# Layer 0's first norm: root on ScalarE, norm weights through TensorE, loads in another order

## The chip, the core and the metric

The kernel runs on one core of one Trainium2 chip. The metric is device time in microseconds (us) of one execution, given as the median of several runs. TensorE (PE, its weight loads PEld) multiplies matrices, VectorE (DVE) and ScalarE (ACT) do elementwise work, GpSimd (POOL) does some more of it, SyncE (SP) issues most DMAs. Every engine takes its instructions strictly in the order of the program and waits on semaphores for the others.

## The reference, cut to what matters

Two layers over 1024 tokens of width 1024: layer 0 mixes by neighbourhood attention, layer 1 by grouped-query attention. Each starts with an RMS norm and a projection. The change touches only the first norm and what surrounds it:

```
def rms_norm(x, g):
    y = x * lax.rsqrt(mean(x * x, axis=-1, keepdims=True) + NORM_EPS)
    return y * g

for i in range(DEPTH):
    h = rms_norm(x, norm_g[i])          # i == 0: the norm of this case
    y = mixer_a(h, ...)                 # layer 0: q, k, v, gate = split(h @ w_in, 4)
    ...
```

## The kernel before

All matrix products are done in three parts: every f32 operand is split into a high part (`wh`, `HTh`) and the rest (`wl`, `HTl`), and `split3` multiplies high by high, high by low and low by high. `mixer_a` begins with a prologue that this case is about. The 1024 tokens are eight tiles `X[t]` of 128 tokens by 1024 columns. For each tile:

- `square` (L720, ACT) makes the sum of squares of each token in a column of `stat`; an ACTIVATE and a short read of the accumulator.
- `newton` (L723) and `rsqrt_ops` (L308) make the reciprocal root on DVE: a shift and a subtraction on the bits for a first guess, then three Newton steps, 10 or 13 instructions of one to four columns each. They run for tile 0, tile 1, tiles 2 and 3, and tiles 4 to 7 as groups; `weave` lays them between other work.
- `scale` (L734) multiplies the tile by root and norm weight. Tiles 0, 1, 2, 4 and 6 do it in one DVE instruction against `gt`, the norm weights copied to all 128 partitions by a DMA of 512 KB (L745). Tiles 3, 5 and 7 do it in two: ACT by the root (L738), POOL by the weights (L739).
- `to_ht` (L422) transposes the tile in two halves of four PE transposes (L427) into a PSUM tile `t`, copies it to `HTh` (L428, ACT) and the rest to `HTl` (L429, DVE).
- `v_items` (L582) projects it to v for the first four heads: two halves of four column blocks, 12 matmuls each (L302), first against weight unit `("av", 0, 0)`, then `("av", 0, 1)`. The evacuation of the PSUM tile `d` takes ACT (L587) and DVE (L588).

The class `Weights` (`WQ`) brings weights in: `stage` issues the DMA of a unit of 512 KB into one of two staging tiles (L202, SP), `pump` copies it to `wh` on ACT (L217) and leaves the subtraction for `wl` (L218, DVE) to `settle`. The order of all of it is the order in which this code is written (the schedule is manual): each call appends to its engine's queue. The SP queue holds tile 0, the 512 KB of norm weights, tile 1, two weight units, tiles 2 to 7. After the eight tiles come `qk_items(0)` (512-column matmuls) and the attention loop, whose scores take the PSUM pool `psS`.

Of the kernel before, what the change touches and what calls it, by code (L numbers as in the profile page):

```python
# [11 lines left out]
F32 = mybir.dt.float32  # L12
# [24 lines left out]
DT = (5, 2)  # L37
FIN = (4, 4)
HOLD = 2
DP = 1  # L40
KD, KS = 3, 4
QD = (2, 5, 8)
# [42 lines left out]
def lay_out(inp):  # L85
    g = {k: np.asarray(v) for k, v in inp.items()}
    W = np.empty((len(UNIT), 128, 1024), np.float32)

    def put(keys, cols, per):
        blk = cols.reshape(cols.shape[0] // 128, 128, -1).transpose(1, 0, 2)  # L90
        for u, key in enumerate(keys):
            W[UNIT[key]] = blk[:, u * per:(u + 1) * per].reshape(128, -1)

    aq, ak, av, ag = np.split(g["a_w_in"][0], 4, axis=1)
    for h in range(16):
        s = slice(h * HD, (h + 1) * HD)
        put([("aqk", h)], np.concatenate([aq[:, s], ak[:, s]], axis=1), 8)
    for q in range(4):
        put([("av", q, 0), ("av", q, 1)], av[:, q * 256:(q + 1) * 256], 4)
    bw = g["b_w_in"][0]  # L100
    bq, bk, bv, bg = bw[:, :1024], bw[:, 1024:1280], bw[:, 1280:1536], bw[:, 1536:]
    for p in range(8):
        s = slice(p * 128, (p + 1) * 128)
        put([("ag", p)], ag[:, s], 8)
        put([("bg", p)], bg[:, s], 8)
    for i in range(4):
        put([("bq", i, 0), ("bq", i, 1)], bq[:, i * 256:(i + 1) * 256], 4)
    for i in range(2):
# [12 lines left out]
    rpb = np.zeros((16, 31, 32), np.float32)  # L121
    rpb[:, 8:23, :31] = g["a_rpb"][0]

    gains = np.stack([g["norm_g"][0], g["ple_norm_g"][0], g["norm_g"][1], g["ple_norm_g"][1], g["final_norm_g"]])

    r = np.arange(128) // 8
    c = np.arange(128) % 8
    rs = np.clip(r - 4, 0, 8)
    rowok = (r[None, :] >= rs[:, None]) & (r[None, :] < rs[:, None] + 8)
    left = rowok & (c[None, :] >= c[:, None])  # L130
    right = rowok & (c[None, :] < c[:, None])
    ok = np.stack([rowok, left, rowok, right, rowok], axis=1)
    mask = np.where(ok, 0.0, BIG).astype(np.float32)

    inv = np.power(np.float32(10000.0), -np.arange(16, dtype=np.float32) * np.float32(2.0) / np.float32(32.0)).astype(np.float32)
    row = r.astype(np.float32)[:, None, None] + np.zeros((1, 8, 1), np.float32)
    col = (8 * np.arange(8)[None, :] + c[:, None]).astype(np.float32)[:, :, None]
    ar = (row * inv).astype(np.float32)
    ac = (col * inv).astype(np.float32)
    cosT = np.concatenate([np.cos(ar), np.cos(ar), np.cos(ac), np.cos(ac)], axis=2).astype(np.float32)  # L140
    sinT = np.concatenate([-np.sin(ar), np.sin(ar), -np.sin(ac), np.sin(ac)], axis=2).astype(np.float32)

    def swap(v):
        return v.reshape(2, 2, 16)[:, ::-1].reshape(64)

    bqn, bkn = g["b_q_norm"][0], g["b_k_norm"][0]
    hg = np.stack([bqn, swap(bqn), bkn, swap(bkn)])
    return {
        "x": tokens(g["x"][0]), "wts": W, "rpb": rpb, "gains": gains, "hgains": hg,
        "mask": mask, "rope": np.stack([cosT, sinT], axis=1),  # L150
    }


@with_exitstack
def trunk(ctx, tc, x, wts, rpb, gains, hgains, mask, rope, out):
    nc = tc.nc
    sync, act, dve, pool, pe = nc.sync, nc.scalar, nc.vector, nc.gpsimd, nc.tensor

# [218 lines left out]
            items.append((f, 650.0 * (k1 - k0)))  # L377
        return items

    def proj_N(keys, t, ncol, alloc, evac, release=(), kstep=None):  # L380
        kstep = kstep or KN
        st = {}
        items = []
        per = 1024 // ncol
        nk = per * len(keys)
        for k0, k1 in chunks(nk, kstep):
            def f(k0=k0, k1=k1):
                if k0 == 0:
                    st["ps"] = alloc()
                for k in range(k0, k1):  # L390
                    wh, wl = WQ.get(keys[k // per])
                    c = slice((k % per) * ncol, (k % per + 1) * ncol)
                    split3(st["ps"], HTh[:, t, k, :], HTl[:, t, k, :], wh[:, c], wl[:, c], k == 0, k == nk - 1)
                if k1 == nk:
                    if release:
                        WQ.done(*release)
                    evac(st["ps"])
            items.append((f, 3 * (ncol / 2.4 + 3) * (k1 - k0)))
        return items
# [160 lines left out]
    def mixer_a():  # L560
        with ExitStack() as es:
# [17 lines left out]
            QS, KA, KB, TB, RS, SP, OP, UT = {}, {}, {}, {}, {}, {}, {}, {}  # L579
            later = Later()  # L580

            def v_items(qd, t):  # L582
                keys = [("av", qd, 0), ("av", qd, 1)]

                def evac(ps):
                    v = ps.rearrange("p (h d) -> p h d", h=4)
                    act.activation(V[:, t, :, 0:64], v, AF.Copy)  # L587
                    dve.tensor_tensor(V[:, t, :, 64:128], v, V[:, t, :, 0:64], ALU.subtract)  # L588
                return [d[0] for d in proj_N(keys, t, 256, valloc, evac, release=keys if t == NT - 1 else ())]

            def qk_evac(h, hf):
                def evac(ps):
# [115 lines left out]
            e2 = es.enter_context(ExitStack())  # L708
            ini = e2.enter_context(tc.tile_pool(name="ini", bufs=1))
            X = [ini.tile([128, D], F32, name=f"X{t}") for t in range(NT)]  # L710
            gt = ini.tile([128, D], F32, name="gain")
            junk = ini.tile([128, D], BF16, name="junk")
            stat = one.tile([128, 3, 8], F32, name="stat")
            wk = one.tile([128, 24], F32, name="wki")
# [1 line left out]
            def load(t):  # L716
                sync.dma_start(X[t], x[t])
# [1 line left out]
            def square(t):  # L719
                act.activation(junk, X[t], AF.Square, accum_out=stat[:, 0, t:t + 1])  # L720

            def newton(a, b):
                ms = stat[:, 1, a:b]  # L723
                return [lambda: dve.tensor_scalar(ms, stat[:, 0, a:b], 1.0 / D, EPS, op0=ALU.mult, op1=ALU.add)] \
                    + rsqrt_ops(stat[:, 2, a:b], ms, wk)

            def weave(ops, fs):
                per = -(-len(ops) // len(fs))
                for i, f in enumerate(fs):
                    for o in ops[i * per:(i + 1) * per]:  # L730
                        o()
                    f()

            def scale(t):  # L734
                if t % 2 == 0 or t == 1:
                    dve.scalar_tensor_tensor(X[t], X[t], stat[:, 2, t:t + 1], gt, op0=ALU.mult, op1=ALU.mult)
                else:
                    act.activation(X[t], X[t], AF.Copy, scale=stat[:, 2, t:t + 1])  # L738
                    pool.tensor_tensor(X[t], X[t], gt, ALU.mult)  # L739

            def ht(t):
                return [lambda c=c: to_ht(psT, t, X[t], (c,)) for c in range(2)]

            load(0)
            sync.dma_start(gt, bcast(gains, 0, D))  # L745
            load(1)
            WQ.stage(True)
            for t in range(2, NT):
                load(t)
            U = dram.tile([16, 8, 31, 24], F32, name="U")  # L750
            square(0)
            square(1)
            weave(newton(0, 1), [lambda: scale(0)])
            WQ.pump(True)
            WQ.pump(True)
            vs = [v_items(0, t) for t in range(NT)]
            weave(newton(1, 2), ht(0))
            scale(1)
            square(2)
            square(3)  # L760
            vs[0][0]()
            weave(newton(2, 4), ht(1))
            scale(2)
            scale(3)
            square(4)
            square(5)
            square(6)
            vs[0][1]()
            sync.dma_start(MK, mask)
            for c in range(8):  # L770
                sync.dma_start(U[:, c], rpb[:, :, 7 - c:31 - c])
            for t in range(1, NT):
                vs[t][0]()
                if t + 1 < NT:
                    weave(newton(4, 8) if t == 2 else [], ht(t + 1))
                if t == 1:
                    square(7)
                if t in (2, 3):
                    scale(2 * t)
                    scale(2 * t + 1)  # L780
                vs[t][1]()
                if t == 6:
                    load_u(0)
# [526 lines left out]
    dense_phase(1)  # L1310


NAMES = ["x", "wts", "rpb", "gains", "hgains", "mask", "rope"]


# [13 lines left out]
```

## Time and profile before

| | us |
|---|---|
| median of 3 runs (1569.87 to 1572.43) | 1572.35 |
| the profiled execution | 1569.38 |
| its span, first to last instruction | 1567.6 |
| PE busy in the span | 1522.6 |
| ACT busy in the span | 871.6 |

The span is read as follows: each row of the timeline gives a start and a duration from the span's start, the engine, the line, what is written from what, and in brackets how long the engine sat idle before and what ended that. Windows give the busy time of each engine in a stretch.

### The profile page before, as it was taken

How to read it: one execution, taken by the hardware profiler on the slowest of the kernel's cores; microseconds unless marked ns; L12 is line 12 of the kernel's file. 1: busy time of each engine (PE TensorE's matmuls, PEld its weight loads, DVE VectorE, ACT ScalarE, POOL GpSimd, SP SyncE). 2: the span in 40 equal slices, each digit the busy share in tenths (PEclk: the TensorE clock that was granted, in tenths of full speed). 3: DMA queues.
4: the chain of work that ended last, by engine and by line, in shares of the span. 5: the costliest groups of instructions: out<-in, count | busy, mean ns of one | idle time of the engine just before them, and what ended most of it. 6: DMA issues, size and time to landing. Idle time of an engine off the chain costs nothing.

```text
span 1567.6 us, 24292 instructions
## 1 busy us (share of the span) xinstructions
PE 1522.6 (97%) x9048; PEld 1328.5 (85%) x9048; DVE 1025.5 (65%) x2062; ACT 871.6 (56%) x1744; POOL 277.3 (18%) x372
## 2 busy tenths in 40 slices
PE   6999999999999999999999999999999999999997
PEld 5888988988988788888988889989899888788886
DVE  6576576477477436547877776777777877625636
ACT  6465465466366522433566776666667767622422
POOL 2111121122112010000312132443132200000023
PEclk9999999999999999999999999999999999999999
DMA  8212122132123972132210111102111213651213
GB/s 273 78 41 74 49 84 78 34 98 78 35 85 95 340 241 67 62 139 90 74 48 21 38 51 41 58 25 68 37 33 42 75 42 112 225 202 54 74 55 128
DMA packets 89861, 138.84 MB, mean 89 GB/s; under 512 B 16912, under 2 KB 55952, under 8 KB 89744
## 3 DMA queue, kind: packets, MB, share of 16 engines
q1 hardware_dynamic: 85136, 122.62, 24.1%
q10 hardware_dynamic: 4608, 14.68, 2.6%
q8 instruction: 71, 1.16, 0.3%
q14 instruction: 46, 0.38, 0.1%
HBM read 104.65 MB, written 36.15 MB: 90 GB/s over the span
## 4 chain that ended last, share of the span: by engine, by line
PE 40%; DVE 7%; ACT 3%; issue 2%; DMA 0%; ACTq 0%; SPq 0%; POOL 0%; DVEq 0%; POOLq 0%
PE d L302 21%; PE o L302 7%; PE t L1084 5%; PE s L302 5%; DVE PTl L1087 2%; DVE mn L1068 1%; ACT PTh L1086 1%; DVE wl L218 1%; PE t L427 1%; ACT wh L217 1%; PE t L1038 0%; ACT P L1074 0%; DVE QS L1048 0%; DVE ss L915 0%; DVE KB L979 0%
## 5 line engine op out<-in xcount | busy, mean ns | idle before, releaser
L302 PE MATMUL d<-wh,HTh 128*128 128x256 f32 (+1 forms) x1096 | 372.5, 340 | 4.6 <-ACT HTh L428 2.1
L302 PE MATMUL d<-wh,HTl 128*128 128x256 f32 (+1 forms) x1096 | 365.8, 334 | 1.6 <-DVE HTl L429 1.5
L302 PE MATMUL d<-wl,HTh 128*128 128x256 f32 (+1 forms) x1096 | 365.3, 333 | 0.0
L1087 DVE TENSOR_TENSOR PTl<-t,PTh 128x512 fp32r<-128x512 f32 x256 | 164.5, 684 | 115.4 <-ACT PTh L1086 114.9
L302 PEld LDWEIGHTS d<-wh,HTh 128*128 128x128 f32 x1096 | 207.9, 190 | 28.0 <-ACT HTh L428 2.7
L302 PEld LDWEIGHTS d<-wh,HTl 128*128 128x128 f32 x1096 | 207.8, 190 | 24.0 <-DVE HTl L429 2.3
L302 PEld LDWEIGHTS d<-wl,HTh 128*128 128x128 f32 x1096 | 208.1, 190 | 21.4
L302 PE MATMUL d<-HTh,wh 128*128 128x512 f32 x504 | 205.9, 409 | 0.0
L302 PE MATMUL d<-HTh,wl 128*128 128x512 f32 x504 | 197.7, 392 | 0.0
L302 PE MATMUL d<-HTl,wh 128*128 128x512 f32 x504 | 197.7, 392 | 0.0
L1074 ACT ACTIVATE P<-s,mn 128x1024 f32<-128x1024 f32 x128 | 142.8, 1115 | 66.2 <-DVE mn L1068 65.1
L302 PE MATMUL o<-PTl,V 128*128 128x256 f32 (+2 forms) x672 | 174.2, 290 | 3.2 <-DVE PTl L1087 2.0
L302 PE MATMUL o<-PTh,V 128*128 128x256 f32 (+2 forms) x672 | 173.0, 288 | 2.3 <-ACT P L1074 1.1
L1086 ACT ACTIVATE PTh<-t 128x512 fp32r<-128x512 f32 x256 | 139.9, 593 | 45.9 <-PE t L1084 45.0
L1068 DVE TENSOR_REDUCE mn<-s 128x1 f32<-128x1024 f32 x128 | 154.8, 1209 | 10.8 <-PE s L302 10.7
L1084 PE MATMUL t<-ident,P 128*128 128x128 f32 x1024 | 137.2, 275 | 8.0 <-DVE PTl L1087 6.6
L218 DVE TENSOR_TENSOR wl<-wstage,wh 128x1024 fp32r<-128x1024 f32 x89 | 115.0, 1298 | 40.9 <-ACT wh L217 40.4
L302 PEld LDWEIGHTS o<-PTl,V 128*128 128x128 f32 x672 | 127.9, 190 | 10.6 <-DVE PTl L1087 6.4
L302 PEld LDWEIGHTS o<-PTh,V 128*128 128x128 f32 x672 | 127.7, 190 | 8.1 <-issue 1.5
L1084 PEld LDWEIGHTS t<-ident,P 128*128 128x128 f32 x1024 | 114.9, 140 | 23.1 <-DVE PTl L1087 16.2
L302 PE MATMUL s<-KA,QS 128*128 128x512 f32 (+2 forms) x384 | 133.6, 402 | 0.0
L302 PE MATMUL s<-KB,QS 128*128 128x512 f32 (+2 forms) x384 | 121.8, 371 | 0.0
(179 smaller groups left out, 2446.8 us busy)
## 6 DMA issues: line engine op xcount, KB each, us to landing
wstage<-in_wts SPq DMA_DIRECT2D x92, 512.0 KB
X<-in_x SPq DMA_DIRECT2D x16, 512.0 KB
pp<-ppD SPq DMA_DIRECT2D x32, 256.0 KB
rb<-rD SPq DMA_DIRECT2D x56, 128.0 KB
ppD<-th SPq DMA_DIRECT2D x20, 256.0 KB
xD<-X SPq DMA_DIRECT2D x8, 512.0 KB
X<-xD SPq DMA_DIRECT2D x8, 512.0 KB
yD0h<-rb SPq DMA_DIRECT2D x14, 256.0 KB
```

The costliest lines, as they stand in the source:

```text
L217: act.activation(hi, s, AF.Copy)
L218: self.rest = lambda: dve.tensor_tensor(lo, s, hi, ALU.subtract)
L302: pe.matmul(ps, a, b, start=first, stop=last, skip_group_check=True)
L427: pe.transpose(ps[:, k], xn[:, (4 * c + k) * 128:(4 * c + k + 1) * 128], ident)
L1068: dve.tensor_reduce(mn, ps, axis=AX.X, op=ALU.min)
L1074: act.activation(p, ps, AF.Exp, bias=mn, scale=-1.0, accum_out=RS[h, hf][:, t:t + 1])
L1084: pe.transpose(ps[:, i], p[:, k * 128:(k + 1) * 128], ident)
L1086: act.activation(PTh[:, ks, c], ps, AF.Copy)
L1087: dve.tensor_tensor(PTl[:, ks, c], ps, PTh[:, ks, c], ALU.subtract)
```

## The change

The first norm takes another way to the root. `chain(a, b)` replaces `newton` and `weave`: ACT computes Ln(sum / 1024 + eps) and Exp of -0.5 times that, DVE adds one Newton step (three or four instructions). It runs once for each of tiles 0 to 3 and once for tiles 4 and 5 and for tiles 6 and 7. `scale` is two DVE instructions of 512 columns for every tile, and reads the norm weights from two PSUM tiles that PE fills: a DMA of 128 x 8 values (`gT`, on ACT's queue), spread over the partitions by eight transposes. `warm` adds eight transposes of the identity before these and eight behind. SP loads tile 0, weight unit 0, tile 1, weight unit 1, tiles 2 to 7. For tiles 0 and 1 the 12 matmuls of a half are ordered by part (`thirds`). Layers, loops and DMAs behind the eight tiles stay in their order on every engine.

```diff
+        "gain0": gains[0].reshape(8, 128).T,
...
-    def proj_N(keys, t, ncol, alloc, evac, release=(), kstep=None):
+    def proj_N(keys, t, ncol, alloc, evac, release=(), kstep=None, thirds=False):
...
+                for i in range(3 if thirds else 0):
+                    for k in range(k0, k1):
...
+                        a, b = ((HTh, wh), (HTh, wl), (HTl, wh))[i]
+                        mm(st["ps"], a[:, t, k, :], b[:, c], i == 0 and k == 0, i == 2 and k == nk - 1)
...
+            def chain(a, b):
+                n = b - a
+                ss, y, r = stat[:, 0, a:b], stat[:, 1, a:b], stat[:, 2, a:b]
+                h, w = wk[:, a:b], wk[:, 8 + a:8 + b]
+                act.activation(w, ss, AF.Ln, scale=1.0 / D, bias=eps)
+                act.activation(y, w, AF.Exp, scale=-0.5)
+                dve.tensor_scalar(h, ss, -0.5 / D, -0.5 * EPS, op0=ALU.mult, op1=ALU.add)
...
+                dve.scalar_tensor_tensor(r, w, 1.5, y, op0=ALU.add, op1=ALU.mult)
+
+            def scale(t, cs=(0, 1)):
+                for c in cs:
+                    w = slice(512 * c, 512 * c + 512)
+                    dve.scalar_tensor_tensor(X[t][:, w], X[t][:, w], stat[:, 2, t:t + 1], gain[c], op0=ALU.mult, op1=ALU.mult)
...
+            def warm(ps, n):
+                for k in range(n):
+                    pe.transpose(ps[:, k % 4 * 128:k % 4 * 128 + 128], ident, ident)
...
+            act.dma_start(gT, gain0)
+            hold = WQ.hold
+            WQ.hold = ("av", 0, 1)
             load(0)
-            sync.dma_start(gt, bcast(gains, 0, D))
+            WQ.stage(True)
             load(1)
+            WQ.hold = hold
             WQ.stage(True)
             for t in range(2, NT):
                 load(t)
...
+            dve.memset(eps, EPS)
+            act.activation(junk[:, :1], eps, AF.Ln)
+            gain = [psS.tile([128, 512], F32, name="s") for c in range(2)]
+            warm(gain[0], WARM[0])
+            for k in range(KC):
+                pe.transpose(gain[k // 4][:, k % 4 * 128:k % 4 * 128 + 128], gT[:, k:k + 1].to_broadcast([128, 128]), ident)
+            warm(pd.tile([128, 512], F32, name="d"), WARM[1])
...
             square(0)
+            chain(0, 1)
+            scale(0)
+            split()
+            ht(0, (0,))
             square(1)
+            chain(1, 2)
+            ht(0, (1,))
             scale(1)
+            vs[0][0]()
+            split()
             square(2)
+            chain(2, 3)
+            ht(1)
+            scale(2)
             square(3)
+            chain(3, 4)
+            vs[0][1]()
+            vs[1][0]()
+            ht(2, (0,))
+            vs[1][1]()
+            ht(2, (1,))
             scale(3)
...
-            for t in range(1, NT):
+            for t in range(2, NT):
                 vs[t][0]()
                 if t + 1 < NT:
-                    weave(newton(4, 8) if t == 2 else [], ht(t + 1))
+                    ht(t + 1)
...
                 if t in (2, 3):
-                    scale(2 * t)
-                    scale(2 * t + 1)
+                    square(2 * t)
+                    square(2 * t + 1)
+                    chain(2 * t, 2 * t + 2)
+                if t + 2 < NT:
+                    scale(t + 2)
                 vs[t][1]()
```

ACT's queue at tiles 0 and 1. `X_107` and `X_108` are the tiles 0 and 1, `X_109` is tile 2; `junk,stat` is the square, `wki<-stat,eps` the logarithm, `stat<-wki` the exponential, ACT_TABLE_LOAD an instruction that the build puts in for the function that follows. Before:

```order
L720 ACTIVATE junk,stat<-X_107 128x1024
L720 ACTIVATE junk,stat<-X_108 128x1024
L217 ACTIVATE wh_146<-wstage 128x1024
L217 ACTIVATE wh_152<-wstage 128x1024
L428 ACTIVATE HTh<-t 128x512 x2
L720 ACTIVATE junk,stat<-X_109 128x1024
```

And of the change:

```order
L729 ACTIVATE junk,stat<-X_107 128x1024
L735 ACTIVATE wki<-stat,eps 128x1
L736 ACT_TABLE_LOAD
L736 ACTIVATE stat<-wki 128x1
L219 ACTIVATE wh_171<-wstage 128x1024
L436 ACTIVATE HTh<-t 128x512
L729 ACTIVATE junk,stat<-X_108 128x1024
L735 ACT_TABLE_LOAD
L735 ACTIVATE wki<-stat,eps 128x1
L736 ACT_TABLE_LOAD
L736 ACTIVATE stat<-wki 128x1
L436 ACTIVATE HTh<-t 128x512
```

Tile 0's second half (the last row) now stands behind tile 1's square, two table loads, the logarithm and the exponential.

ACT's queue at tiles 4 to 7 (`X_111` to `X_114`), from the square of tile 4. Before, the squares of tiles 4 to 6 follow each other, and one root serves all four:

```order
L720 ACTIVATE junk,stat<-X_111 128x1024
L720 ACTIVATE junk,stat<-X_112 128x1024
L720 ACTIVATE junk,stat<-X_113 128x1024
L587 ACTIVATE V<-d 128x4x64
L428 ACTIVATE HTh<-t 128x512 x2
L720 ACTIVATE junk,stat<-X_114 128x1024
```

And of the change:

```order
L729 ACTIVATE junk,stat<-X_111 128x1024
L729 ACTIVATE junk,stat<-X_112 128x1024
L735 ACT_TABLE_LOAD
L735 ACTIVATE wki<-stat,eps 128x2
L736 ACT_TABLE_LOAD
L736 ACTIVATE stat<-wki 128x2
L595 ACTIVATE V<-d 128x4x64
L436 ACTIVATE HTh<-t 128x512 x2
L729 ACTIVATE junk,stat<-X_113 128x1024
```

The same group of two squares, two loads, logarithm and exponential follows once more for tiles 6 and 7. In all ACT has one ACT_TABLE_LOAD before and twelve now, the first of them in front of the logarithm of `eps` at the start; none stands behind the eight tiles.

DVE's queue of the change at the root of tiles 6 and 7, up to the scaling of tile 5 (`X_112`):

```order
L596 TENSOR_TENSOR V<-d,V 128x4x64
L437 TENSOR_TENSOR HTl<-t,HTh 128x512 x2
L737 TENSOR_SCALAR wki<-stat 128x2
L742 TENSOR_TENSOR wki<-stat 128x2
L743 TENSOR_TENSOR wki<-wki 128x2
L744 SCALAR_TENSOR_TENSOR stat<-wki,stat 128x2
L749 SCALAR_TENSOR_TENSOR X_112<-X_112,stat,s 128x512 x2
```

Tile 5 is scaled behind the Newton step of tiles 6 and 7, which reads their exponential.

More of the change, by code (lines that the diff above doesn't have):

```diff
@@ L39 @@
 HOLD = 2
+WARM = (8, 8)
 DP = 1
@@ L150, in lay_out, with trunk @@
         "mask": mask, "rope": np.stack([cosT, sinT], axis=1),
+        "gain0": gains[0].reshape(8, 128).T,
     }
 @with_exitstack
-def trunk(ctx, tc, x, wts, rpb, gains, hgains, mask, rope, out):
+def trunk(ctx, tc, x, wts, rpb, gains, hgains, mask, rope, gain0, out):
     nc = tc.nc
@@ L389, in f @@
                     st["ps"] = alloc()
-                for k in range(k0, k1):
+                for i in range(3 if thirds else 0):
+                    for k in range(k0, k1):
+                        wh, wl = WQ.get(keys[k // per])
+                        c = slice((k % per) * ncol, (k % per + 1) * ncol)
+                        a, b = ((HTh, wh), (HTh, wl), (HTl, wh))[i]
+                        mm(st["ps"], a[:, t, k, :], b[:, c], i == 0 and k == 0, i == 2 and k == nk - 1)
+                for k in range(k0, k1) if not thirds else ():
                     wh, wl = WQ.get(keys[k // per])
@@ L580, in mixer_a, with v_items @@
             later = Later()
-            def v_items(qd, t):
+            def v_items(qd, t, thirds=False):
                 keys = [("av", qd, 0), ("av", qd, 1)]
@@ L588, in evac @@
                     dve.tensor_tensor(V[:, t, :, 64:128], v, V[:, t, :, 0:64], ALU.subtract)
-                return [d[0] for d in proj_N(keys, t, 256, valloc, evac, release=keys if t == NT - 1 else ())]
+                return [d[0] for d in proj_N(keys, t, 256, valloc, evac, release=keys if t == NT - 1 else (), thirds=thirds)]
             def qk_evac(h, hf):
@@ L710, in mixer_a @@
             X = [ini.tile([128, D], F32, name=f"X{t}") for t in range(NT)]
-            gt = ini.tile([128, D], F32, name="gain")
+            gT = ini.tile([128, 8], F32, name="gT")
+            eps = ini.tile([128, 1], F32, name="eps")
             junk = ini.tile([128, D], BF16, name="junk")
@@ L720, in square @@
                 act.activation(junk, X[t], AF.Square, accum_out=stat[:, 0, t:t + 1])
[L722 to L732, printed above, removed]
@@ L734, in scale @@
-            def scale(t):
-                if t % 2 == 0 or t == 1:
-                    dve.scalar_tensor_tensor(X[t], X[t], stat[:, 2, t:t + 1], gt, op0=ALU.mult, op1=ALU.mult)
-                else:
[L738 to L742, printed above, removed]
+            def chain(a, b):
[5 more added lines that the diff above has]
+                dve.tensor_scalar(h, ss, -0.5 / D, -0.5 * EPS, op0=ALU.mult, op1=ALU.add)
+                w = wk[:, 16 + a:16 + b]
+                if n == 1:
+                    dve.scalar_tensor_tensor(w, y, h, y, op0=ALU.mult, op1=ALU.mult)
+                else:
+                    dve.tensor_tensor(w, y, y, ALU.mult)
+                    dve.tensor_tensor(w, w, h, ALU.mult)
+                dve.scalar_tensor_tensor(r, w, 1.5, y, op0=ALU.add, op1=ALU.mult)
@@ new lines, in scale, with ht, split @@
+            def scale(t, cs=(0, 1)):
+                for c in cs:
+                    w = slice(512 * c, 512 * c + 512)
+                    dve.scalar_tensor_tensor(X[t][:, w], X[t][:, w], stat[:, 2, t:t + 1], gain[c], op0=ALU.mult, op1=ALU.mult)
+            def ht(t, cs=(0, 1)):
+                to_ht(psT, t, X[t], cs)
+            def warm(ps, n):
+                for k in range(n):
+                    pe.transpose(ps[:, k % 4 * 128:k % 4 * 128 + 128], ident, ident)
+            def split():
+                WQ.pump(True)
+                WQ.settle()
@@ L744, in mixer_a @@
+            U = dram.tile([16, 8, 31, 24], F32, name="U")
+            act.dma_start(gT, gain0)
+            hold = WQ.hold
+            WQ.hold = ("av", 0, 1)
             load(0)
-            sync.dma_start(gt, bcast(gains, 0, D))
+            WQ.stage(True)
             load(1)
+            WQ.hold = hold
             WQ.stage(True)
@@ L749, in mixer_a @@
                 load(t)
-            U = dram.tile([16, 8, 31, 24], F32, name="U")
+            dve.memset(eps, EPS)
[5 more added lines that the diff above has]
+            warm(pd.tile([128, 512], F32, name="d"), WARM[1])
+            vs = [v_items(0, t, t < 2) for t in range(NT)]
             square(0)
+            chain(0, 1)
+            scale(0)
+            split()
+            ht(0, (0,))
             square(1)
[L753 to L757, printed above, removed]
+            chain(1, 2)
+            ht(0, (1,))
             scale(1)
+            vs[0][0]()
+            split()
             square(2)
+            chain(2, 3)
+            ht(1)
+            scale(2)
             square(3)
-            vs[0][0]()
-            weave(newton(2, 4), ht(1))
-            scale(2)
+            chain(3, 4)
[4 more added lines that the diff above has]
+            ht(2, (1,))
             scale(3)
[L765 to L768, printed above, removed]
             sync.dma_start(MK, mask)
@@ L771, in mixer_a @@
                 sync.dma_start(U[:, c], rpb[:, :, 7 - c:31 - c])
-            for t in range(1, NT):
+            for t in range(2, NT):
                 vs[t][0]()
                 if t + 1 < NT:
-                    weave(newton(4, 8) if t == 2 else [], ht(t + 1))
-                if t == 1:
-                    square(7)
+                    ht(t + 1)
                 if t in (2, 3):
-                    scale(2 * t)
-                    scale(2 * t + 1)
+                    square(2 * t)
[3 more added lines that the diff above has]
+                    scale(t + 2)
                 vs[t][1]()
@@ L1310, in trunk @@
     dense_phase(1)
-NAMES = ["x", "wts", "rpb", "gains", "hgains", "mask", "rope"]
+NAMES = ["x", "wts", "rpb", "gains", "hgains", "mask", "rope", "gain0"]
 def kernel(**inputs):
```

## The prediction

> **What bounds the kernel now.** I read the page first, then the windows of the first 60 us, then the timeline of each engine there, because the order of the instructions behind the eight tiles is the same before and after.
>
> ```profile
> span 1567.6 us, 24292 instructions
> ...
> PE 1522.6 (97%) x9048; PEld 1328.5 (85%) x9048; DVE 1025.5 (65%) x2062; ACT 871.6 (56%) x1744; POOL 277.3 (18%) x372
> ```
>
> PE is busy 97% of the span, so behind the prologue there is little slack that could swallow a delay: what the prologue gains or loses arrives at the end nearly whole. The windows give start, end and length, then the busy time of PE, PEld, DVE, ACT and POOL, the granted clock, DMA share and GB/s:
>
> ```profile
> 8.00:18.00 10.00, 7.66 (x32) 6.72 (x33) 8.27 (x24) 7.20 (x12) 0.00 (x0) 1.00 1.03 414
> 18.00:24.00 6.00, 5.14 (x42) 4.76 (x41) 2.91 (x9) 4.70 (x9) 2.71 (x1) 1.00 0.77 145
> 24.00:40.00 16.00, 12.67 (x102) 12.12 (x103) 13.76 (x29) 10.77 (x19) 5.94 (x2) 1.00 0.76 229
> 40.00:49.70 9.70, 9.70 (x84) 9.70 (x84) 4.92 (x9) 2.94 (x6) 2.15 (x5) 1.00 0.36 126
> 49.70:60.60 10.90, 10.90 (x50) 9.03 (x49) 4.92 (x7) 4.14 (x6) 1.43 (x4) 1.00 0.33 115
> ```
>
> PE does nothing in the first 8.9 us, is fed in pieces until 40 us, and from there is the bound (9.70 of 9.70). ACT has 7.20 of 10, 4.70 of 6 and 10.77 of 16 us: the engine with most work per tile beside DVE, and with about 9 us free between 8 and 40. That room is what the change spends.
>
> ```profile
> 0.71 1.28 ACT L720 ACT_TABLE_LOAD   x1 [0.71 <-PEq L1321]
> 4.32 1.06 ACT L720 ACTIVATE junk<-X 128x1024 bf16<-128x1024 f32 x1 [2.32 <-DMA X<-in_x]
> 5.28 0.19 ACT L720 ACTIVATION_READ_ACCUMULATOR junk<-X 128x1 f32 x1
> 5.50 0.15 DVE L724 TENSOR_SCALAR stat<-stat 128x1 f32<-128x1 f32 x1 [5.50 <-ACT junk L720]
> ...
> 7.27 0.16 DVE L324 SCALAR_TENSOR_TENSOR stat<-wki 128x1 f32<-128x1 f32 x1
> 7.47 1.28 DVE L736 SCALAR_TENSOR_TENSOR X<-X,stat,gain 128x1024 f32<-128x1024 f32 x1
> 8.90 1.94 PE L427 MATMUL t<-ident,X 128*128 128x128 f32 x8 [8.90 <-DVE X L736]
> ...
> 13.75 0.41 PE L302 MATMUL d<-wh,HTh 128*128 128x256 f32 x1
> 13.97 0.41 PE L302 MATMUL d<-wl,HTh 128*128 128x256 f32 x1
> ...
> 18.33 0.29 PE L302 MATMUL d<-wh,HTh 128*128 128x256 f32 x1
> 18.46 0.28 PE L302 MATMUL d<-wl,HTh 128*128 128x256 f32 x1
> ...
> 49.71 0.40 PE L302 MATMUL d<-HTh,wh 128*128 128x512 f32 x1
> ```
>
> The timeline (start, duration, engine, line): the root of tile 0 takes DVE from 5.50 to 7.43, scaling to 8.75, and PE starts at 8.90. PE's early matmuls start 0.22 us apart, from 18 us on 0.12, though the granted clock reads 1.00 in all these windows. The last row, at 49.71, is the first matmul behind the eight tiles: my yardstick.
>
> **The change part by part.** The order shows one table load before and twelve now. The first falls, as before, into the wait for tile 0. Eleven lie between a square and what needs its root. So I follow ACT's queue from the arrival of tile 0 (4.32) to the exponential of tiles 6 and 7, behind which nothing waits for a load. The prices:
>
> ```profile
> L720 ACT ACT_TABLE_LOAD x1 | 1.3, 1283 | 0.7 <-PEq L1321 0.7
> L720 ACT ACTIVATION_READ_ACCUMULATOR junk<-X 128x1 f32 x8 | 1.5, 191 | 0.0
> L217 ACT ACTIVATE wh<-wstage 128x1024 fp32r<-128x1024 f32 x6 | 6.2, 1056 | 0.3 <-DMA wstage<-in_wts 0.2
> ...
> 20.45 1.04 ACT L720 ACTIVATE junk<-X 128x1024 bf16<-128x1024 f32 x1
> 21.61 1.06 ACT L720 ACTIVATE junk<-X 128x1024 bf16<-128x1024 f32 x1
> 23.85 0.36 ACT L587 ACTIVATE V<-d 128x256 fp32r<-128x256 f32 x1
> 24.11 1.08 ACT L428 ACTIVATE HTh<-t 128x512 fp32r<-128x512 f32 x2
> 24.25 0.42 DVE L588 TENSOR_TENSOR V<-d,V 128x256 fp32r<-128x256 f32 x1 [3.16 <-ACT V L587]
> 24.73 1.29 DVE L429 TENSOR_TENSOR HTl<-t,HTh 128x512 fp32r<-128x512 f32 x2
> ```
>
> - 8 squares, 1.17 apart (21.61 less 20.45): 9.4.
> - 11 table loads at 1.283: 14.1.
> - 6 logarithms and 6 exponentials of one or two columns. No row shows one; the read of one column is 0.19, a 256-column copy 0.36. I take 0.20, near the first, since the size is: 2.4.
> - 2 weight copies at 1.06: 2.1. Ten halves of `HTh` (tiles 0 to 4) at 0.54: 5.4. Evacuations of V for tiles 0 to 2 at 0.36: 1.1.
>
> Sum 34.5. To it come ACT's own waits in this order. For tile 0's transposes: the weight copy ends at 8.3, scaling gives its first half at 8.4, the four transposes 9.1: 0.8. For tile 3: behind the exponential DVE has two small steps (0.5), the two V subtractions (0.8), two halves of `HTl` (1.3) and a half scaling (0.64), then PE four transposes (0.5) and 0.2 of handing over, 3.9, of which ACT fills 1.8 with two V and two `HTh`: 2.1. For tile 4: three small steps (0.6), half a scaling (0.64), transposes (0.5), handing over 0.3, less one V: 1.7. Together 4.6, so the last exponential ends at 4.3 + 34.5 + 4.6 = 43.4.
>
> Tile 5 is scaled behind it on DVE: 0.6 + 0.64 + 0.3, its transposes start at 44.9. From there PE is the bound again: three tiles' transposes and seven halves of 12 matmuls.
>
> ```profile
> 21.23 1.07 PE L427 MATMUL t<-ident,X 128*128 128x128 f32 x8 [0.59 <-DVE X L736]
> 24.82 0.35 PE L302 MATMUL d<-wh,HTh 128*128 128x256 f32 x1 [1.09 <-ACT HTh L428]
> 31.72 1.06 PE L427 MATMUL t<-ident,X 128*128 128x128 f32 x8 [1.04 <-DVE X L736]
> 43.29 0.38 ACT L587 ACTIVATE V<-d 128x256 fp32r<-128x256 f32 x1 [0.78 <-PE d L302]
> 47.03 0.38 ACT L587 ACTIVATE V<-d 128x256 fp32r<-128x256 f32 x1 [0.78 <-PE d L302]
> ```
>
> Transposes take 1.06; a whole tile 3.74 (47.03 less 43.29), so a half is (3.74 - 1.06) / 2 = 1.34, up to 12 x 0.12 = 1.44. 3 x 1.06 + 7 x 1.4 = 13.0, and about 0.7 of short waits for `HTl` and scaling, which share DVE with two weight subtractions: the first 512-column matmul comes at 58.6 in place of 49.71, **+8.9**.
>
> Three costs the rows don't fix. What a load costs beyond its 1.28 between other work: nothing, or at most a whole square with its read (1.15) if the queue must run empty first. A dependent pair in this trace has little between them:
>
> ```profile
> 55.38 0.60 ACT L601 ACTIVATE th<-d 128x512 f32<-128x512 f32 x1 [3.19 <-PE d L302]
> 56.05 0.63 ACT L604 ACTIVATE QS<-th 64x512 fp32r<-64x512 f32 x1
> ```
>
> That is 0.07, the nearest row, and I take it: 11 x 0.07 = 0.8 (bound 12.7). The twelve small activations at 0.36 instead of 0.20 would add 1.9; I take none. And PE will stand idle for about 4 us each in front of the transposes of tiles 1, 4 and 5, where the trace has gaps of 1.09 and 1.04 once it is fast (rows 24.82 and 31.72), which leave the spacing at 0.12, and some 9 us of slow spacing behind its first idle of 8.9 us (8.90 to before 18.33). Nothing, or 9 us at 0.22 in place of 0.12 from tile 5 on (4.1 lost) plus tile 4's transposes at 1.94 (0.9): about 5.0. I take 1.0, as the gaps are nearer to 1 us than to a cold start. None of the three can be below nothing: each price in the list is already the shortest that a row shows.
>
> The rest I cost at nothing, with its cover:
> - Norm weights by PE: 24 transposes at 0.24 are 5.8 us, from about 1.3 to 7.1, under the wait for tile 0's scaling at 8.4. If `gT` landed as late as tile 0 did (4.3), the last 16 end at 8.2; without that cover the first transposes would start up to 1 us later, and ACT with them.
> - SP: weight unit 0 goes where 512 KB of norm weights went, the tiles behind come 512 KB sooner; nobody waits for them, as ACT reaches each square after it has landed. Mask and bias DMAs keep their places; their user on POOL runs at 45.55 for scores at 60.62, 13 us of room, and moves with the rest:
>
> ```profile
> 45.55 2.15 POOL L635 TENSOR_TENSOR tb<-MK,u 128x128 f32<-128x128 f32 x5 [7.80 <-DMA u<-U]
> 60.62 0.28 PE L302 MATMUL s<-KA,QS 128*128 128x256 f32 x1
> ```
>
> - Newton on DVE goes from 10 to 3 steps: tile 0's root is ready at 7.7 (square 5.47, logarithm, load, exponential 7.2, two steps), not 7.43, and scaling by halves lets PE begin at 8.5, not 8.90. This 0.4 is in the sum.
> - POOL loses three multiplications and ACT three scalings (left out of the list above), DVE gains three scalings of 1.28:
>
> ```profile
> L739 POOL TENSOR_TENSOR X<-X,gain 128x1024 f32<-128x1024 f32 x3 | 8.6, 2882 | 27.8 <-ACT X L738 27.8
> L738 ACT ACTIVATE X<-X,stat 128x1024 f32<-128x1024 f32 x3 | 3.5, 1154 | 2.6 <-DVE stat L324 2.6
> ```
>
> The sum: 8.9 + 0.8 + 1.0 = **+10.7**. Against the profiled execution (1569.38, of which 1.8 lies outside its span) that is 1580.1; the median of the runs is 3.0 higher, so 1572.35 + 10.7 = **1583**.
>
> **Rivals.**
> - *The loads are dearer.* Each must let the queue run empty: up to 1.15 more, 11 x 1.15 = 12.7 in place of 0.8, 22.6 in all: 1595. For it: no load in this trace has work in front of it. Against: one-column instructions are in front of half of them, and those are done in 0.2. The Trainium skill speaks for it (ScalarE: Activation LUTs, section What ACT_TABLE_LOAD costs): about 1283 ns for the load, which agrees with the 1283 of the row here, and 1380 ns more for a drain, 2.66 us a switch; by that the sum would be +26 (11 x 1.38 = 15.2 on 10.7). No run here shows the drain.
> - *Faster: the loads don't bind.* If logarithm and exponential were served without a change of table, ACT's queue would be 14.1 shorter: the last exponential would come at 31.3 (43.4 - 14.1 + 2.0 of waits that then open for DVE and PE), tile 5 at 32.8, the yardstick at 46.5, -3.2, and the time 1569. It decides from about 0.4 us a load downwards. For it: the root's DVE chain is really shorter, and POOL's multiplications go. Against it stand the two load rows of every chain in the order, and the load's 1.28 in the trace. The Trainium skill has a rule for it (the same page, section Table sets: the hidden batching unit): ln followed by exp needs one load, since one set holds both. The order of the changed kernel differs from it: it loads for each of the two.
> - *The delay is swallowed*: the stages behind wait for DMAs anyway, and the end moves by under 3 us, about 1574. PE's 97% speaks against it; a load that starts later because its issue stands behind the prologue moves too.
>
> **How the numbers follow.** Forecast 0.75, dearer loads 0.14, faster 0.06, swallowed 0.05. The forecast's own range is 1579 (my waits counted too high by 4) to 1590 (small activations 1.9 and cold PE 5.0 in full). To hold 8 in 10 it reaches into the dearer case: 1577 to 1596. A measurement here tells 0.2%, 3.1 us, from no change: faster 0.06, same 0.04 (most of the swallowed case), slower 0.90.
>
> **What would show it.** Right: twelve ACT_TABLE_LOAD rows of about 1.28 in the first 45 us, ACT busy almost without a break between 4 and 43 us, PE idle for 4 us with ACT or DVE's scaling as releaser in front of tiles 1, 4 and 5, and the first 512-column matmul near 59 to 61. Dearer loads would show as idle time of ACT around each load; the faster rival as fewer than twelve load rows or far shorter ones, and that matmul near 46. Wrong in size: matmuls 0.22 apart behind the gaps add what I have put at 1.0. If that matmul is late by what I say and the span is not, the delay was swallowed.

## The result, and the profile after

| | us |
|---|---|
| before, median of 6 runs (1569.77 to 1573.78) | 1571.56 |
| changed, median of 6 runs (1580.2 to 1584.21) | 1580.67 |
| ratio changed to before | 1.0064, 95% interval 1.0053 to 1.0075 |
| the profiled execution of the changed kernel | 1584.21, span 1582.4 |

The change makes the kernel slower by about 10 us (the interval is 8 to 12); the medians are 9.1 apart. The profiled execution is the slowest of the six. Two single executions far off the rest, one of the kernel before at 5336 us and one of the run e3 below at 5605 us, stand outside all ratios. First the page, then the same windows as before (start and end, length, busy PE, PEld, DVE, ACT, POOL, granted clock, DMA share, GB/s):

```profile
span 1582.4 us, 24350 instructions
...
PE 1534.0 (97%) x9072; PEld 1338.5 (85%) x9072; DVE 1026.8 (65%) x2048; ACT 884.7 (56%) x1765; POOL 269.1 (17%) x369
```

```profile
8.00:18.00 10.00, 4.96 (x30) 4.23 (x30) 6.85 (x12) 8.82 (x13) 0.00 (x0) 0.83 1.06 392
18.00:24.00 6.00, 6.00 (x39) 5.92 (x39) 3.04 (x7) 5.92 (x10) 0.00 (x0) 0.72 0.75 137
24.00:40.00 16.00, 10.03 (x67) 9.07 (x66) 8.61 (x19) 10.90 (x20) 0.00 (x0) 0.84 0.63 194
40.00:49.70 9.70, 6.62 (x36) 6.44 (x36) 5.15 (x12) 7.12 (x12) 0.00 (x0) 0.68 0.06 21
49.70:60.60 10.90, 10.90 (x86) 10.90 (x86) 7.35 (x12) 4.27 (x8) 2.15 (x5) 0.89 0.28 99
```

ACT goes from 7.20 to 8.82 of 10 us in the first window and from 4.70 to 5.92 of 6 in the second: full. PE falls from 7.66 to 4.96, and in 40 to 49.7, where it had been the bound (9.70), it works 6.62. The second window shows 6.00 of 6 for PE with 39 matmuls instead of 42: there it is slow, at a granted clock of 0.72. The page as a whole says little: PE has the same 97%.

Why ACT is full stands in its timeline, here from the read of tile 1's square to the copy of tile 0's second half:

```profile
10.91 0.19 ACT L729 ACTIVATION_READ_ACCUMULATOR junk<-X 128x1 f32 x1
11.12 1.28 ACT L735 ACT_TABLE_LOAD   x1
12.42 0.29 ACT L735 ACTIVATE wki<-stat,eps 128x1 f32<-128x1 f32 x1
12.73 1.28 ACT L736 ACT_TABLE_LOAD   x1
14.02 0.20 ACT L736 ACTIVATE stat<-wki 128x1 f32<-128x1 f32 x1
14.13 0.58 ACT L436 ACTIVATE HTh<-t 128x512 fp32r<-128x512 f32 x1
```

One root costs ACT 3.01 us (11.12 to 14.13), of which 2.57 is two loads. They stand against each other with 0.01 to 0.02 between rows. The groups, costliest first (busy us, mean ns, idle time in front):

```profile
L736 ACT ACT_TABLE_LOAD x6 | 7.7, 1283 | 0.1
L735 ACT ACT_TABLE_LOAD x5 | 6.4, 1283 | 0.1
...
L735 ACT ACTIVATE wki<-stat,eps 128x1 f32<-128x1 f32 (+1 forms) x6 | 1.8, 295 | 0.1
...
L736 ACT ACTIVATE stat<-wki 128x1 f32<-128x1 f32 (+1 forms) x6 | 1.2, 203 | 0.1
```

Eleven loads, 14.1 us. What that does to PE, in its timeline (transposes of tiles 1, 4 and 5, then the first matmul behind the eight tiles), with ACT's last exponential:

```profile
16.19 1.94 PE L435 MATMUL t<-ident,X 128*128 128x128 f32 x8 [4.27 <-issue]
36.89 1.94 PE L435 MATMUL t<-ident,X 128*128 128x128 f32 x8 [4.58 <-issue]
44.60 0.20 ACT L736 ACTIVATE stat<-wki 128x2 f32<-128x2 f32 x1
46.15 1.94 PE L435 MATMUL t<-ident,X 128*128 128x128 f32 x8 [3.08 <-issue]
61.55 0.40 PE L304 MATMUL d<-HTh,wh 128*128 128x512 f32 x1
```

The yardstick is 11.84 us late (61.55 for 49.71). The delay then travels on unchanged. The first and the 14th multiplication by the gate on POOL in layer 0, before:

```profile
111.65 1.29 POOL L513 TENSOR_TENSOR Y<-Y,G 128x512 f32<-128x512 f32 x1 [1.33 <-DVE Y L443]
...
487.02 1.79 POOL L513 TENSOR_TENSOR Y<-Y,G 128x512 f32<-128x512 f32 x1 [3.21 <-DVE Y L443]
```

and after:

```profile
123.45 1.30 POOL L521 TENSOR_TENSOR Y<-Y,G 128x512 f32<-128x512 f32 x1 [1.33 <-DVE Y L451]
...
498.85 1.79 POOL L521 TENSOR_TENSOR Y<-Y,G 128x512 f32<-128x512 f32 x1 [3.05 <-DVE Y L451]
```

11.80 and 11.83 late, 375 us apart: nothing swallows it. The stretch from the 14th to the end of the span took 1083.6 us here and 1081.0 in another execution of the same kernel (e10), 1080.6 before. Single executions differ there by more than the prologue's smaller effects, so a span is a poorer measure of the prologue than the yardstick.

### The profile page after: what moved, and what is told of

The parts are those of the page before. It is cut to its first block, busy times and chain, and to the rows that moved or that the text cites. A ratio compares the mean times of both kernels' runs of the same rounds, so it can differ in the third digit from the quotient of the medians.

```text
span 1582.4 us, 24350 instructions
## 1 busy us (share of the span) xinstructions
PE 1534.0 (97%) x9072; PEld 1338.5 (85%) x9072; DVE 1026.8 (65%) x2048; ACT 884.7 (56%) x1765; POOL 269.1 (17%) x369
## 3 DMA queue, kind: packets, MB, share of 16 engines
q8 instruction: 71, 1.16, 0.3%
## 4 chain that ended last, share of the span: by engine, by line
PE 40%; DVE 7%; ACT 3%; issue 2%; DMA 0%; ACTq 0%; SPq 0%; POOL 0%; DVEq 0%; POOLq 0%
PE d L304 21%; PE o L304 8%; PE t L1120 5%; PE s L304 5%; DVE PTl L1123 2%; DVE mn L1104 1%; ACT PTh L1122 1%; PE t L435 1%; DVE wl L220 1%; PE t L1074 1%; ACT wh L219 0%; ACT P L1110 0%; DVE QS L1084 0%; DVE KB L1015 0%; DVE Y L451 0%
## 5 line engine op out<-in xcount | busy, mean ns | idle before, releaser
L1104 DVE TENSOR_REDUCE mn<-s 128x1 f32<-128x1024 f32 x128 | 154.7, 1208 | 10.8 <-PE s L304 10.7
L304 PEld LDWEIGHTS o<-PTl,V 128*128 128x128 f32 x672 | 128.1, 191 | 10.7 <-DVE PTl L1123 6.4
```

What stands on the lines that cost most here:

```text
L304: pe.matmul(ps, a, b, start=first, stop=last, skip_group_check=True)
L1104: dve.tensor_reduce(mn, ps, axis=AX.X, op=ALU.min)
```

## The experiments

Ratios are to the kernel before, with 95% intervals; an edit is against the changed kernel unless said otherwise. "Yardstick" is the start of the first 512-column matmul in that run's profile: 49.71 before, 61.55 changed.

### e1: the logarithm replaced, one load left

```diff
-                act.activation(w, ss, AF.Ln, scale=1.0 / D, bias=eps)
+                act.activation(w, ss, AF.Identity, scale=1.0 / D, bias=eps)
...
-            act.activation(junk[:, :1], eps, AF.Ln)
+            act.activation(junk[:, :1], eps, AF.Exp)
```

> The changed kernel with the logarithm replaced by Identity (same shape, scale and bias), so that the root is not the reference's; every other instruction stays, and of the twelve table loads one is left. Theory (the eleven loads between square and root bind, ACT's queue being the path): ACT's queue is 11 x 1.28 = 14.1 us shorter, tile 5 is scaled before 34 us, the first 512-column matmul behind the eight tiles comes near 47 in place of 61.6, and the time is 1 to 5 us below the kernel before. Rival (the new order on ACT, the scaling against PSUM or PE's slow spells bind, the loads lie in waits): that matmul stays behind 58 and the time 6 to 12 us above before.

Ratio 0.9987 (0.9978 to 0.9996), 2 us below before; the yardstick in its profile:

```profile
47.87 0.40 PE L304 MATMUL d<-HTh,wh 128*128 128x512 f32 x1
```

The number of activations, their order and the way of the norm weights are those of the changed kernel; only the loads are gone. PE's gaps in front of tiles 1, 4 and 5 shrink to 1.8 to 2.0 us with them. The loss of 10 us becomes a gain of 2. The theory holds, and the rival that blamed the order or the scaling falls.

### e2: a root whose functions need no switch

```diff
-                act.activation(w, ss, AF.Ln, scale=1.0 / D, bias=eps)
-                act.activation(y, w, AF.Exp, scale=-0.5)
+                act.activation(w, ss, AF.Sqrt, scale=1.0 / D, bias=eps)
+                dve.reciprocal(y, w)
...
-            act.activation(junk[:, :1], eps, AF.Ln)
+            act.activation(junk[:, :1], eps, AF.Sqrt)
```

> The changed kernel with another way to the same root: ACT's Sqrt, a reciprocal on DVE, then the same Newton step. Two table loads in all, the second at the first exponential of the attention. Theory (table switches are the whole loss): like e1, 1 to 5 us below before, the first 512-column matmul near 47, with one load of 1.28 near its end where PE is the bound. Rival (ScalarE in the root is the loss, whatever the table): 5 us or more above before.

Ratio 0.9988 (0.9979 to 0.9997), 2 us below before, yardstick 47.65. ACT's timeline at the same place as above, and its one more load:

```profile
10.43 0.19 ACT L729 ACTIVATION_READ_ACCUMULATOR junk<-X 128x1 f32 x1
10.65 0.29 ACT L735 ACTIVATE wki<-stat,eps 128x1 f32<-128x1 f32 x1
10.86 0.58 ACT L436 ACTIVATE HTh<-t 128x512 fp32r<-128x512 f32 x1
...
61.78 1.28 ACT L677 ACT_TABLE_LOAD   x1
```

The root costs ACT 0.21 instead of 3.01. Squares, copies and Sqrt run under one load, and the one that returns to the exponential comes at 61.78, where PE is the bound. ScalarE in the root is not the loss, the switches are.

### e6: twelve more loads

```diff
                 act.activation(y, w, AF.Exp, scale=-0.5)
+                act.activation(junk[:, :1], eps, AF.Ln)
+                act.activation(junk[:, :1], eps, AF.Exp)
```

> The changed kernel with one more logarithm and exponential of one column behind each exponential, whose results nobody reads: twelve more table loads, 24 in all. Theory (each load is paid in full on the path): 12 x (1.28 + about 0.25) = 18 us more than the changed kernel, 27 above before. Rival (part of a load hides in a wait, or PE takes over as the bound): under 12 us more.

Ratio 1.0155 (1.0140 to 1.0170); against the change's 1.0064 that is 0.0091, 14 us more (about 11 to 17 with both intervals), for 18 expected by the one theory and under 12 by the other. The yardstick is 12.1 us behind the changed kernel's, so the loads are not paid in full. Six pairs are 6 x 3.01 = 18.1 us on ACT; ACT's wait in front of tile 4's copy shows where some of it went. In the changed kernel, then here:

```profile
38.01 0.60 ACT L436 ACTIVATE HTh<-t 128x512 fp32r<-128x512 f32 x1 [2.32 <-PE t L435]
```

```profile
50.28 1.08 ACT L436 ACTIVATE HTh<-t 128x512 fp32r<-128x512 f32 x2
```

The added loads lie behind the exponential, while DVE and PE work on what it gave: there they first fill the 2.3 us for which ACT had waited, and likewise 1.1 us at tile 0. Tile 5's transposes here (the yardstick follows at 73.63):

```profile
58.05 1.50 PE L435 MATMUL t<-ident,X 128*128 128x128 f32 x8 [3.94 <-issue]
```

For five pairs, 15.1 us, tile 5's transposes come 11.9 later than in the changed kernel (58.05 for 46.15): the two waits account for the difference. The sixth pair stands behind the exponential that tile 5 waits for, and from those transposes to the yardstick it adds 0.2 (15.6 for 15.4). A load between a square and its root has less cover: without eleven of them, 14.1 us, the yardstick came 13.7 earlier in e1, part of it through PE's pace.

### e5, e10 and e11: PE kept at work in its gaps

e5 and e11 are the same kernel, e10 is the changed kernel again, on the same chip as e11.

```diff
+            def fill(n):
+                o = psO.tile([128, 512], F32, name="o")
+                for k in range(n):
+                    mm(o, HTh[:, 0, 0, :], HTh[:, 0, 0:4, :], True, True)
...
+            fill(16)
             ht(1)
...
+                if t in (3, 4):
+                    fill(16)
                 if t + 1 < NT:
                     ht(t + 1)
```

> The changed kernel with 16 more matmuls of 512 columns, whose result nobody reads, in front of the transposes of tiles 1, 4 and 5, where PE sat idle for 4 us. Theory (PE's slow spacing behind those gaps costs part of the 9 us): the transposes of tiles 1, 4 and 5 take 1.07 in place of 1.94, and the time falls by 1 to 3 us from the changed kernel, to 6 to 8 above before. Rival (PE's pace is hidden behind ACT's queue): within 0.5 us of the changed kernel, 9 to 10 above before, or later if the fillers last too long.

> The changed kernel once more, on the same chip and beside the next, since one profile each left the fillers' worth open: the profile of the change has PE's first 512-column matmul at 61.55 and slow transposes of 1.94 for tiles 1, 4 and 5. If the slow spells come back in every run, the same three transposes take 1.94 again and that matmul comes at 61 to 62; if they vary from run to run, it comes anywhere from 59.7 on. Time 9 to 10.5 above before.

> The kernel of e5 once more. Theory (the slow spells cost about 1.8 us, which the first profile of e5 gained in the prologue): 1 to 2.5 us below the changed kernel in the same job. Rival (nothing, as the medians of the first jobs had it): within 0.7 us of it.

Ratios: e5 1.0068 (1.0056 to 1.0080), e10 1.0064 (1.0050 to 1.0077), e11 1.0064 (1.0051 to 1.0077); the medians of e10 and e11 are 1580.97 and 1581.06. In time the fillers bring nothing that can be told, so both forecasts of a gain were missed. PE's timeline in e10, tiles 4 and 5 and the yardstick:

```profile
36.92 1.94 PE L435 MATMUL t<-ident,X 128*128 128x128 f32 x8 [4.58 <-issue]
46.18 1.80 PE L435 MATMUL t<-ident,X 128*128 128x128 f32 x8 [2.60 <-issue]
...
60.46 0.40 PE L304 MATMUL d<-HTh,wh 128*128 128x512 f32 x1
```

and in e11:

```profile
37.82 1.33 PE L435 MATMUL t<-ident,X 128*128 128x128 f32 x8 [0.92 <-issue]
46.48 1.33 PE L435 MATMUL t<-ident,X 128*128 128x128 f32 x8 [0.80 <-issue]
...
59.92 0.40 PE L304 MATMUL d<-HTh,wh 128*128 128x512 f32 x1
```

The same rows in e5:

```profile
37.66 1.33 PE L435 MATMUL t<-ident,X 128*128 128x128 f32 x8 [0.93 <-issue]
46.31 1.33 PE L435 MATMUL t<-ident,X 128*128 128x128 f32 x8 [0.80 <-issue]
...
59.75 0.40 PE L304 MATMUL d<-HTh,wh 128*128 128x512 f32 x1
```

The fillers do what they should to the transposes (1.33, though not the 1.07 expected; scaling now feeds them in halves). From tile 4's transposes to the yardstick the changed kernel takes 24.66 us in its first profile and 23.54 in e10, the filled kernel 22.09 and 22.10. So the slow pace behind the gaps is real and costs the prologue 2.6 us in one execution and 1.4 in the other. The yardstick moves by less, 1.8 and 0.5, largely because tile 0 came later to the filled kernel: the first square starts at 5.18 and 5.00 in e5 and e11, at 4.44 and 4.46 in the two profiles of the changed kernel. Whether the fillers have to do with that, and whether the time gains anything, these runs don't show.

### e3 and e12: the root on DVE, all else as changed

e12 is the kernel of e3 again, a single execution, for its profile.

```diff
+                ms = stat[:, 1, a:b]
+                dve.tensor_scalar(ms, stat[:, 0, a:b], 1.0 / D, EPS, op0=ALU.mult, op1=ALU.add)
+                rsqrt(stat[:, 2, a:b], ms, wk)
...
-                act.activation(w, ss, AF.Ln, scale=1.0 / D, bias=eps)
-                act.activation(y, w, AF.Exp, scale=-0.5)
```

> The changed kernel's order, loads and norm weights by PE, with the root on DVE as before (first guess from the bits, three Newton steps), one table load. Theory (without table loads the way of the root is worth under 2 us; the rest of the change gives about 2): the first 512-column matmul at 48 to 50, the time 2 below to 0.5 above before. Rival (the DVE root is what held the prologue before): later than 50.5, at or above before.

> The kernel of e3 once more, for its profile. Theory (DVE, not ACT, holds this prologue: the root adds 1.5 us to each of six chains and stands in front of HTl and scaling): PE's waits in front of the transposes are released by DVE, and the first 512-column matmul comes at 52 to 54, as the time of e3 has it. Rival (the 3.6 us of e3 arose behind the prologue): it comes before 50.5.

Ratio of e3 1.0023 (1.0014 to 1.0032), 3.6 us above before; my theory of "2 below to 0.5 above" falls. The windows of e12:

```profile
8.00:18.00 10.00, 6.94 (x40) 6.22 (x41) 9.42 (x29) 6.33 (x11) 0.00 (x0) 0.83 1.05 393
18.00:24.00 6.00, 5.58 (x45) 5.00 (x44) 5.72 (x19) 1.96 (x4) 0.00 (x0) 1.00 0.67 130
...
53.48 0.40 PE L304 MATMUL d<-HTh,wh 128*128 128x512 f32 x1
```

DVE is nearly full (9.42 of 10, 5.72 of 6) and the yardstick 3.77 late, all of the loss. Six chains of 10 or 13 steps stand on DVE in one piece in front of `HTl` and scaling; before, four chains were laid between other work, and POOL and ACT scaled three tiles. Scaling all eight tiles on DVE is not what costs, for e2 does that too and is 2 us below before. So the way of the root is worth 5.8 us between e2 and e12 by the yardstick, not under 2. Part of it is PE's slow pace, which comes back here too: tile 4's transposes take 1.94 behind 3.24 us of idle time.

### e7 and e8: the transposes of the identity, the norm weights and loads

Both start from e2. e7 sets `WARM = (0, 0)`. e8 brings the norm weights by the DMA of before:

```diff
-            act.dma_start(gT, gain0)
-            WQ.hold = ("av", 0, 1)
             load(0)
-            WQ.stage(True)
+            sync.dma_start(gt, bcast(gains, 0, D))
             load(1)
...
+            gain = [gt[:, 512 * c:512 * c + 512] for c in range(2)]
```

> The kernel of e2 without the 16 transposes of the identity. Theory (PE's pace at tile 0 and 1 lies under ACT and DVE): within 0.7 us of e2, the first 512-column matmul between 47 and 48.4. Rival (a slow PE at the start delays the first copies, and so all of ACT's queue): 1 to 2 us later than e2.

> The kernel of e2 with the norm weights by the 512 KB DMA as before, and SP's loads in the order of before; no transposes for the weights, scaling against SBUF. Theory (the first weight unit lands one or two 512 KB transfers later and ACT copies it before tile 0's HTh): the first 512-column matmul 1 to 3 us later than in e2, the time about that of before. Rival (the loads are hidden anyway, and scaling against SBUF takes 1.28 in place of 1.40): 0.5 to 1 us below e2.

e7: ratio 0.9987 (0.9978 to 0.9996), yardstick 47.58, as e2: the 16 transposes change nothing that shows. e8: ratio 0.9992 (0.9983 to 1.0001), yardstick 49.56, 1.9 later than e2. Its ACT timeline has the first half of the cause:

```profile
9.07 1.06 ACT L219 ACTIVATE wh<-wstage 128x1024 fp32r<-128x1024 f32 x1 [3.23 <-DMA wstage<-in_wts]
```

ACT waits 3.23 us for the first weight unit, with tile 0's copies behind it; in e2 that copy ran at 5.88. The other half stands at tile 5. PE's rows for tiles 4 and 5 and the yardstick in e8, and for tile 5 in e2:

```profile
29.10 1.33 PE L435 MATMUL t<-ident,X 128*128 128x128 f32 x8 [1.99 <-issue]
35.17 1.80 PE L435 MATMUL t<-ident,X 128*128 128x128 f32 x8 [1.86 <-issue]
...
49.56 0.40 PE L304 MATMUL d<-HTh,wh 128*128 128x512 f32 x1
```

```profile
34.22 1.33 PE L435 MATMUL t<-ident,X 128*128 128x128 f32 x8 [0.49 <-issue]
```

Tile 4 is 1.08 later than in e2 (29.10 for 28.02, shown under e9) and tile 5 0.95; only behind it, where PE ran at its slow pace, does the difference grow to 1.9. By these rows the later weight unit costs 1.0 to 1.1 us, not 1.9. Whether the slow pace behind tile 5 comes from the edit or only from this execution, one profile doesn't show; the ratios of e2 and e8 overlap. Scaling against SBUF took 1.41 for two halves, as against PSUM (1.40), so the rival's saving isn't there: it is two instructions that make 1.28 into 1.40.

### e9: squares of tiles 4 to 7 earlier

Against e2:

```diff
-                if t + 1 < NT:
-                    ht(t + 1)
                 if t in (2, 3):
                     square(2 * t)
                     square(2 * t + 1)
                     chain(2 * t, 2 * t + 2)
+                if t + 1 < NT:
+                    ht(t + 1)
```

> The kernel of e2 (Sqrt, reciprocal, two loads) with the squares and roots of tiles 4 to 7 ahead of the preceding tile's transposes and copies. In e2 PE still waits 2 us for tile 4 and 0.5 us for tile 5, whose squares stand on ACT behind the copies of tiles 3 and 4. Theory (what is left is the order on ACT): these waits go, the first 512-column matmul comes at 45 to 46.5 in place of 47.65, and the time is 1 to 3 us below e2, 3 to 5 below before. Rival (DVE is the bound from tile 3 on, with scaling, HTl, V and weights 4 us a tile): within 0.7 us of e2.

Ratio 0.9963 (0.9949 to 0.9977), about 6 us below before. Tile 4's transposes and the yardstick in e2, then in e9:

```profile
28.02 1.47 PE L435 MATMUL t<-ident,X 128*128 128x128 f32 x8 [1.98 <-issue]
...
47.65 0.40 PE L304 MATMUL d<-HTh,wh 128*128 128x512 f32 x1
```

```profile
26.08 1.09 PE L435 MATMUL t<-ident,X 128*128 128x128 f32 x8
...
43.96 0.40 PE L304 MATMUL d<-HTh,wh 128*128 128x512 f32 x1
```

The wait of 1.98 is gone, the yardstick 3.7 ahead of e2 and 5.75 ahead of before, more than I expected (45 to 46.5, and 3 to 5 us below before). This kernel is faster than the kernel before, the changed one and e2, whose interval lies above its own.

## Why the prediction was right, by its steps

- *The path.* ACT's queue from tile 0 to the exponential of tiles 6 and 7: right, and shown by e1. It ended at 44.8; the sum had 43.4, or 44.2 with the 0.8 for pauses.
- *The loads.* Eleven at 1.283: measured eleven at 1.283. Beside other work each takes 0.02 more, not the 0.07 that I took, and far from the 1.15 of the rival with dearer loads. The drain of 1380 ns that the Trainium skill adds to a switch (ScalarE: Activation LUTs, What ACT_TABLE_LOAD costs) does not appear: a switch took 1.30, row to row.
- *Small activations.* 0.20 each: the exponential took 0.203, the logarithm 0.295. Since each row's end overlaps the next row, a whole root cost 3.01 from start to start, 0.44 more than its two loads. Loads, pauses and small activations together took 16.8 us (five roots of 3.01 and the first of 1.71), where the sum had 17.3.
- *ACT's waits.* 4.6 in the sum; the rows have 1.10, 2.31 and 2.32 in front of tiles 0, 3 and 4 and 0.26 between tile 4's halves, 6.0. Half of the difference is tile 4, whose transposes ran at the slow pace: in e5, where they did not, ACT waited 1.86 there.
- *Slow PE.* 1.0, between 0 and 5.0: 2.6 in the first profile and 1.4 in e10, by the filled kernels. The term was too small. The gaps were 4.27, 4.58 and 3.08 us, near the 4 that I forecast, and PE came back slow from all three.
- *The tail.* From tile 5's transposes to the yardstick 14.7 predicted with the 1.0 for slow PE, 15.4 in the first profile (46.15 to 61.55) and 14.3 in e10 (46.18 to 60.46). Where PE kept its pace it took 13.4 (e1, e2, e5 and e11), for 13.7 predicted.
- *The sum.* Yardstick predicted 10.7 late, measured 11.8 and 10.75; time predicted 1583, measured 1580.67, a loss of 8 to 12 us by the ratio. That it came out so near is partly luck: waits and slow PE were put too low, roots and tail too high. Two small slips in the working change nothing: the rows 20.45 and 21.61 are 1.16 apart, not 1.17, and the upper end of my own range counts the 1.0 for slow PE twice (1583 + 1.9 + 4.0 is 1589).
- *The delay arrives whole*: 11.80 and 11.83 at POOL's rows, as said; the swallowed rival falls.
- *The faster rival* had its mechanism right and its condition unmet: with the loads gone e1 came out 2 us faster, where I had worked out 3.2. The Trainium skill's rule behind it (the same page, Table sets: the hidden batching unit) differs from this trace: each logarithm but the first and each exponential had a load of its own in front.
- *Covered edits.* The 16 transposes of the identity cost nothing (e7). The new loads and norm weights were not nothing where ACT has room (at least 1.0 in e8); what they are worth in the changed kernel itself no run shows. No run gives POOL and ACT their scalings back either, so that term was only argued.

## What to carry to other kernels

Before ScalarE takes over a few small steps, count the table loads that the build puts in the order, and ask of each whether the path runs through it: here 0.5 us of useful work per root came with 2.6 us of loads. A function that shares a load with what runs around it (Sqrt beside squares and copies here) gives the same root at a fourteenth of ACT's time, with one reciprocal more on DVE. A delay in a prologue in front of a stage that one engine fills is not made good later: here 11.8 us of it were still there at 499 us.

## What the runs showed of the hardware that was not expected

The granted clock shows the slow spells behind gaps (0.83, 0.72, 0.84 and 0.68 in the first four windows of the changed kernel), but it read 1.00 from 8 to 18 us in the kernel before, where matmuls also started 0.22 apart: there the spacing told it, not the clock. How long PE sat idle does not by itself tell whether it comes back slow. Eight transposes took 1.94 behind 3.08 to 4.58 us of idle time in the changed kernel, and 1.33 to 1.47 behind 1.68 and 1.98 in e2. But in e8 they took 1.33 behind 1.99 and 1.80 behind 1.86, with the matmuls that follow 0.12 apart after the first and 0.21 after the second. What decides it stays open.
